# Ten feed-forward input blocks with a fifth seven-product pair, and four weight sums by adding transfers

## The chip, the cores and the metric

The kernel runs on one core of a Trainium2 chip. A core has a matrix engine (TensorE, PE in the profile, with PEld for its weight loads), a vector engine (VectorE, DVE), a scalar engine (ScalarE, ACT), a general engine (GpSimd, POOL) and an engine for synchronisation (SyncE, SP), which here issues the plain transfers. Sixteen DMA engines move the data. SBUF and PSUM are the core's on-chip memories; matmuls write to PSUM, in banks of 128 x 512 float32. The metric is device time in microseconds for one call, smaller is better; the time of a kernel is the median of its runs.

## The reference, cut to what matters

An encoder block on 256 tokens of width 2048, all in float32: three token mixers side by side (one of them attends to 256 memory tokens), an output projection, and a SwiGLU feed-forward part.

```python
h = rms_norm(x, g_mix)
proj = h @ w_in                       # q, k, v of three mixers, and gates
mkv = rms_norm(mem, g_mem) @ w_mem_kv # keys and values of the memory
...
merged = gates[0] * (oa @ w_br_a) + gates[1] * (ob @ w_br_b) + gates[2] * (oc @ w_br_c)
x = x + merged @ w_o
hf = rms_norm(x, g_ffn) @ w_ffn_in                              # 2048 -> 2 * 5632
x = x + (silu(hf[..., :D_FF]) * hf[..., D_FF:]) @ w_ffn_out     # 5632 -> 2048
```

## The kernel before

**Number format.** A float32 product is done as three matmuls of a faster format: each operand is split into a high part (a rounded copy, made by ACT) and a low part (the rest, made by a DVE subtraction), and the kernel sums high x high, high x low and low x high. In `mul` (line 476) these are the three matmuls of one 128-row k-tile, one 128-token tile and 512 columns. Weights are split on the chip, as they arrive: `halves` (line 425) makes the high part of a 512 KB tile (ACT, line 438), and `low` (line 445) issues the subtraction (DVE, line 448) one step later.

**Weights.** They come in tiles of 512 KB: two k-tiles of 128 rows by 512 columns, u = 0 to 7 for a width of 2048. `load` (line 218) takes the first of a list of free places (eleven once `more` and `both` are there) and issues the transfer on SP's queue, in program order; `release` appends the place to the list once the tile's last split has been issued, and a transfer into it waits for that split. Split tiles have five buffers. A weight tile that needs adding to another gets that by an accumulating transfer, which GpSimd's queue issues (line 535): the second matrix is read from memory and added to what lies in the tile.

**Pairs of column blocks.** From the gates on, `pair` (line 450) computes two neighbouring column blocks at once, c = 0 and 1, for both token tiles: a 2 x 2 arrangement of outputs. `whole` (line 499) is the ordinary product of one weight tile with both token tiles: four k-tile products, 12 matmuls. A "double" takes two weight tiles u and their k-tiles in a 2 x 2 form and does, for two pairs of k-tiles at once, seven products in place of eight (Strassen's method in Winograd's form). The seven are called X, W, P, Y, Q, Z, H; each is 6 matmuls for the double. Their weight operands are b11, a sum t = b11 + b12 (the accumulating transfer), then P: t + b22 (DVE, line 581), Y: b21, Q: t - b11 (line 583), Z: b22, H: t + b21 (line 585). In an FFN input block two doubles (u = 0 to 3) are done so, u = 4 to 7 as wholes; it has 28 + 32 = 60 k-tile products of three matmuls. Sums of the banks between the phases are lines 558 to 567.

**Order.** A string lists the steps of a pair, such as

```python
STEPS_FFN = ("l0 l1 X0 X1 . r0 W0 r1 W1 P0 P1 . Y0 Y1 . Q0 Q1 .", "Z0 Z1 D4 H0 D5 H1 D6 D7", "d4 d5 d6 d7")
```

l0 and l1 load b11 and t and issue t's accumulating transfer; r0 and r1 load b22 and b21; D and d are wholes of column blocks 1 and 0. The third string is the tail: its steps take the dots of the next pair's first string, so that the end of a block lies among the beginning of the next. `run` (line 616) takes the steps in this order: a step's weights are made ready (sums, ACT's high part, the deferred low part), and its matmuls are issued four steps later. ACT, DVE and PE run these instructions in the order written.

**FFN.** `feeding` runs input blocks 0 to 3, two output pairs, blocks 4 to 7, two output pairs, blocks 8 to 10, two output pairs. An input block computes 512 columns of both halves of the SwiGLU, then silu (line 983), the product with the other half (line 986), transposes and a split into `hT`. The seven products also need sums of the activations; `transposed` and `token_sums` make them into `room` for the doubles.

**The beginning.** The first products are the memory's keys and values, then the queries, keys and values of x (`whole_k`, all wholes). The two column blocks of these use banks of tags "at" and "tp". `take_slots` (line 656) takes them out of PSUM: keys at once, values (`V`, lines 135 and 136, split straight out of PSUM) only once the row scale r is known, which needs rows that are loaded later. `load_T` (line 261) fetches the transposed inputs, 256 KB for two k-tiles, the first one in two halves of 128 KB between the halves of the first weight tile. Eight matmuls of an identity matrix run on PE ahead of the first product.

**Slots.** Small things (rows, one-hot tables, copies of banks, av) take one of five slots of 4 KB per partition, the s4 pool.

Of the kernel before, what the change touches and what calls it, by code (L numbers as in the profile page):

```python
# [18 lines left out]
P = 128  # L19
# [41 lines left out]
STEPS_FFN = ("l0 l1 X0 X1 . r0 W0 r1 W1 P0 P1 . Y0 Y1 . Q0 Q1 .", "Z0 Z1 D4 H0 D5 H1 D6 D7", "d4 d5 d6 d7")  # L61
STEPS_LAST = ("l0 l1 X0 X1 . r0 W0 . r1 W1 . P0 P1 . Y0 Q0 Q1 Y1", "Z0 Z1 H0 H1 D4 D5", "d4 d5")
# [41 lines left out]
def encoder_block(ctx: ExitStack, tc: tile.TileContext, a: dict, out: bass.AP):  # L104
# [111 lines left out]
    def load(src, k0, nk, parts=1, between=None):  # L216
# [5 lines left out]
        for k in range(0, nk, nk // parts):  # L222
            n = nk // parts
            if k and between:
                between(k0 + k)
            nc.sync.dma_start(out=raw[:, k:k + n].rearrange("p k n -> p (k n)"),
                              in_=src[k0 // PK][:, c + k * NC:c + (k + n) * NC])
# [33 lines left out]
    def load_T(src, g, tag):  # L261
# [3 lines left out]
        raws, fetched, have = {}, set(), set()  # L265

        def get(k, fetch=False, n=2):
# [5 lines left out]
            if not fetched.intersection(ks):  # L273
                nc.sync.dma_start(out=raws[k0][:, ks[0] - k0:ks[0] - k0 + n],
                                  in_=src[k0 // 2].rearrange("p (k s) -> p k s", s=S)[:, ks[0] - k0:ks[0] - k0 + n])
            fetched.update(ks)
# [26 lines left out]
    def transposed(src, dst, g=None, lag=1, also=None):  # L303
# [3 lines left out]
        for h in range(2):  # L307
# [14 lines left out]
            if also is not None:  # L322
# [5 lines left out]
                else:  # L328
                    for k in range(2):
                        nc.scalar.activation(to[:, k], of[:, k], AF.Copy, scale=g(2 * h + k))  # L330
        if also is not None:
            token_sums(full, also)

    def token_sums(full, to):


        raw = s4([P, 2, 4, P], "fraw")
# [12 lines left out]
    for _ in range(8):  # L350
# [74 lines left out]
    def halves(*srcs, each=None):  # L425
# [5 lines left out]
        n = 0  # L431
        for v in srcs:
            v = v.unsqueeze(1) if len(v.shape) == 2 else v
            o = slice(n, n + v.shape[1])
            if each:
                low(0)
                each(n)
            nc.follow(nc.scalar.activation(hi[:, o], v, AF.Copy))  # L438
            due.append((lo[:, o], v, hi[:, o].bitcast(F32)))
# [5 lines left out]
    def low(n):  # L445

        while len(due) > n:
            nc.follow(nc.vector.tensor_sub(*due.pop(0)))  # L448

    def pair(src, lhs, lists, done, doubles=(), forms=None, operand=None, fresh="", early=False, by_halves=False):  # L450
# [12 lines left out]
        left = {"Y": 2 * nd + 2 * wholes["d"], "X": 6 * nd, "V": 2 * nd + 2 * wholes["d"],  # L463
                "W": 4 * nd + 2 * wholes["D"], "Q": 2 * wholes["D"]}
# [3 lines left out]
        stops = {"X": [left["X"] - n * nd for n in (2, 4, 6)], "W": [left["W"] - 2 * nd]}  # L468
# [30 lines left out]
        def whole(u, c):  # L499
            def ready():  # L500
                last_kind[0] = ""
                parts = 2 if operand and u + c == 0 else 1
                if operand and c == 0:
                    operand(2 * u, True, 3 - parts)
                raw = load((src(u, c),), 0, PK, parts, lambda k: operand(k, True, 1))
# [31 lines left out]
        def begin2(m):  # L537
            j = doubles[m][1]
            raws[m].update({"b22": load((src(j, 1),), 0, PK), "b21": load((src(j, 0),), 0, PK)})
# [6 lines left out]
        def phase_end(kind, hi):  # L546
            seen[kind] = seen.get(kind, 0) + 1
            if seen[kind] < nd:
# [19 lines left out]

        def seventh(kind, m):
            of = {"X": "b11", "W": "t", "Y": "b21", "P": "t", "Z": "b22", "Q": "b11", "H": "b21"}[kind]  # L570
            bk = {"P": "X", "Q": "X", "H": ends[0][1], "Z": "W"}.get(kind, kind)
            needs = {"Y": "X", "P": "X", "Z": "P", "Q": "P", "H": "Q"}

            def ready():
                r = raws[m]
                raw = r[of]
# [7 lines left out]
                elif kind == "H":  # L584
                    nc.follow(nc.vector.tensor_add(raw, r["t"], raw))
                hi, lo = halves(raw)
                for n in {"Q": ["b11"], "Z": ["b22"], "H": ["t", "b21"]}.get(kind, ()):
                    release(r.pop(n))

                def products():  # L590
                    assert kind not in needs or seen.get(needs[kind], 0) == nd, (kind, seen)
                    assert kind != "Z" or seen["W"] == nd
                    for i in range(2):
# [4 lines left out]
                        mul(bk, st, hi[:, i], lo[:, i])  # L598
# [5 lines left out]
        def step(o):  # L604
# [5 lines left out]
            if kind in "lr":  # L610
                return lambda: (begin if kind == "l" else begin2)(n)
# [492 lines left out]
```

## Time and profile before

| | |
|---|---|
| Time, median of 3 runs | 1365.81 us (1365.35 to 1368.44) |
| Profiled execution | 1366.78 us, of which the span is 1365.0 us |
| PE busy | 1354.4 us (99%) |
| DVE busy | 1157.6 us (85%) |
| ACT busy | 855.6 us (63%) |
| Transfers | 301.18 MB, 221 GB/s on the mean |
| of them accumulating (queue q0) | 24.12 MB, 9.4% of the DMA engines' span |
| One FFN input block (735.44 to 777.21) | 41.77 us, PE busy throughout |

The span runs from the first to the last instruction of the core; the profiled execution's time has 1.78 us around it. Busy shares are averages over stages that differ. A row of a window lists its bounds and length, then for PE, PEld, DVE, ACT and POOL the busy time with the number of instructions, then PE's granted clock, the busy share of the DMA engines and GB/s. A row of a timeline is start, duration, engine, line, operation, what it writes and reads, and in brackets how long the engine sat idle before it and what it waited for. Matmuls overlap, so that their durations (0.39 us for one of 512 columns) are longer than their distance.

### The profile page before, as it was taken

Reading aid. Unit: us, or ns where it says so; the run is one execution under the profiler, and the core shown is the slowest. Engines: PE = TensorE matmul, PEld = TensorE weight load, DVE = VectorE, ACT = ScalarE, POOL = GpSimd, SP = SyncE. Lnnn points to the kernel's source line nnn. Section 1 sums busy time; section 2 is a strip of 40 time slices with the busy share of each in tenths; the row PEclk is TensorE's granted clock in tenths of the full one; section 3 lists DMA queues with packets and bytes.
Section 4 is the critical chain, followed back from the end, with each engine's and each line's share of the span. In section 5 each row is a group of like instructions: output and inputs, shape, how many; then the busy total and the mean of one; then the engine's idle time right before and its main releaser. Section 6 shows DMA issues by size and latency. Waiting matters only on the chain.

```text
span 1365.0 us, 17319 instructions
## 1 busy us (share of the span) xinstructions
PE 1354.4 (99%) x6170; PEld 1122.6 (82%) x6170; DVE 1157.6 (85%) x1412; ACT 855.6 (63%) x1110; POOL 53.1 (4%) x60
## 2 busy tenths in 40 slices
PE   9989999999999999999999999999999999999998
PEld 7878888888888888888888888888888888888887
DVE  6768876778879779878899998888999889989997
ACT  7766656556656565656776666555666655566664
POOL 0010001000000000000000000000000000000000
PEclk9989999999999999999999999999999999999999
DMA  9967555546785594785578666787666786666873
GB/s 358 351 186 220 155 153 171 171 132 212 256 289 190 183 312 141 264 286 148 191 232 270 187 213 212 244 262 234 202 227 203 249 272 191 227 219 213 278 220 103
DMA packets 86486, 301.18 MB, mean 221 GB/s; under 512 B 9792, under 2 KB 12608, under 8 KB 86144
## 3 DMA queue, kind: packets, MB, share of 16 engines
q1 hardware_dynamic: 79632, 275.94, 58.2%
q0 software_dynamic: 6624, 24.12, 9.4%
q8 instruction: 48, 0.79, 0.2%
q14 instruction: 38, 0.31, 0.1%
q10 hardware_dynamic: 144, 0.02, 0.0%
HBM read 297.17 MB, written 2.88 MB: 220 GB/s over the span
## 4 chain that ended last, share of the span: by engine, by line
PE 94%; DVE 3%; DMA 1%; ACT 1%; issue 1%; SPq 0%; DVEq 0%; ACTq 0%
PE mmX L79 28%; PE mmW L79 19%; PE mm L79 16%; PE mmY L79 15%; PE mmQ L79 11%; DVE wlo L448 2%; PE tp L79 1%; PE sc L79 1%; PE o L79 1%; DMA raw<-in_w_br 1%; ACT whi L438 1%; PE pT L79 1%; PE hT L79 0%; DMA raw<-in_w_mem 0%; DVE raw L583 0%
## 5 line engine op out<-in xcount | busy, mean ns | idle before, releaser
L438 ACT ACTIVATE whi<-raw 128x1024 fp32r<-128x1024 f32 (+1 forms) x363 | 376.9, 1055 | 231.3 <-PE mmQ L79 52.3
L448 DVE TENSOR_TENSOR wlo<-raw,whi 128x1024 fp32r<-128x1024 f32 (+1 forms) x363 | 437.9, 1220 | 84.6 <-ACT whi L438 81.0
L79 PE MATMUL mm<-whi,xT 128*128 128x512 f32 x640 | 205.3, 396 | 3.9 <-DVE V L136 3.9
L79 PEld LDWEIGHTS mm<-whi,xT 128*128 128x128 f32 x640 | 120.6, 190 | 29.3 <-DVE V L136 4.4
L438 ACT ACTIVATE whi<-both 128x1024 fp32r<-128x1024 f32 x101 | 106.5, 1055 | 58.6 <-DVE both L583 18.1
L133 DVE TENSOR_TENSOR wlo<-raw,whi 128x1024 fp32r<-128x1024 f32 x82 | 103.1, 1261 | 42.1 <-ACT whi L132 41.7
L448 DVE TENSOR_TENSOR wlo<-both,whi 128x1024 fp32r<-128x1024 f32 x101 | 123.1, 1222 | 11.6 <-ACT whi L438 10.8
L448 DVE TENSOR_TENSOR wlo<-more,whi 128x1024 fp32r<-128x1024 f32 x89 | 108.7, 1223 | 24.0 <-ACT whi L438 23.0
L438 ACT ACTIVATE whi<-more 128x1024 fp32r<-128x1024 f32 x89 | 93.9, 1058 | 54.2 <-PE mmQ L79 15.4
L79 PE MATMUL mm<-wlo,xT 128*128 128x512 f32 x320 | 126.5, 395 | 0.0
L132 ACT ACTIVATE whi<-raw 128x1024 fp32r<-128x1024 f32 x82 | 86.6, 1061 | 60.4 <-PE mm L79 43.5
L79 PE MATMUL mmW<-whi,forms 128*128 128x512 f32 x368 | 122.1, 391 | 0.0
L79 PE MATMUL mmX<-whi,forms 128*128 128x512 f32 x368 | 122.1, 391 | 0.0
L79 PE MATMUL mmX<-whi,x1T 128*128 128x512 f32 x352 | 120.9, 389 | 0.0
L79 PE MATMUL mmY<-whi,x1T 128*128 128x512 f32 x264 | 89.1, 389 | 0.0
L79 PEld LDWEIGHTS mmW<-whi,forms 128*128 128x128 f32 x368 | 69.1, 188 | 14.2
L79 PEld LDWEIGHTS mmX<-whi,forms 128*128 128x128 f32 x368 | 69.1, 188 | 14.2
L79 PEld LDWEIGHTS mmX<-whi,x1T 128*128 128x128 f32 x352 | 66.1, 188 | 13.7
L79 PE MATMUL mmX<-wlo,forms 128*128 128x512 f32 x184 | 71.7, 389 | 0.0
L79 PE MATMUL mmW<-wlo,forms 128*128 128x512 f32 x184 | 71.7, 389 | 0.0
L79 PEld LDWEIGHTS mm<-wlo,xT 128*128 128x128 f32 x320 | 60.8, 190 | 11.7
L79 PE MATMUL mmX<-wlo,x1T 128*128 128x512 f32 x176 | 68.5, 389 | 0.0
(277 smaller groups left out, 2592.9 us busy)
## 6 DMA issues: line engine op xcount, KB each, us to landing
raw<-in_w_ffn SPq DMA_DIRECT2D x116, 512.0 KB, 5.9
raw<-in_w_gate SPq DMA_DIRECT2D x66, 512.0 KB, 5.0
raw<-in_w_qkv SPq DMA_DIRECT2D x64, 512.0 KB, 4.2
raw<-in_w_ffn_out SPq DMA_DIRECT2D x54, 512.0 KB, 7.1
both<-in_w_ffn SPq DMA_DIRECT2D x33, 512.0 KB, 8.1
more<-in_w_ffn SPq DMA_DIRECT2D x27, 512.0 KB, 6.5
raw<-in_w_o SPq DMA_DIRECT2D x22, 512.0 KB, 4.9
both<-in_w_ffn_out SPq DMA_DIRECT2D x20, 512.0 KB, 5.3
```

Of the source, the lines that this page charges most:

```text
L79: ins = op(*args, **kw)
L132: nc.scalar.activation(hi, src, AF.Copy)
L133: nc.vector.tensor_sub(lo, src, hi.bitcast(F32))
L438: nc.follow(nc.scalar.activation(hi[:, o], v, AF.Copy))
L448: nc.follow(nc.vector.tensor_sub(*due.pop(0)))
```

## The change

Five things change.

1. Ten of the eleven FFN input blocks (n = 1 to 10) get a new step list, `STEPS_FFN5`. In it weight tile u = 6, until now the wholes d6 and D6, becomes a "single": its two k-tiles are one more 2 x 2 form and get seven products in place of eight. They come in four parts, each with its own ready step: S1 (X and W), S2 (P and Y), S3 (Q and Z), S4 (H). Its operands are halves of the two tiles t and b1, and so are its sums (DVE, half tiles) and splits; the sum t is again made by an accumulating transfer, of one half, which step `s0` issues behind its loads. A block then has 59 k-tile products.
2. In these blocks the sum of H of the two doubles is no longer a DVE addition: after Q's subtraction, steps `a0` and `a1` add b21 to t by an accumulating transfer. The tile b21 is loaded at Y instead of at r0 and r1, and given back at once.
3. The activation sums of the single lie in a tile `lone`, which holds one of the s4 slots from the projection to the end. It is filled once, at the last transpose of the projection, by two ACT copies, three small DVE operations and one split.
4. `take_slots` copies the value part of the banks to a tile `vraw` (an s4 slot) at once with two ACT instructions, where the scale is not known yet (the memory's); V is then split from there.
5. `load_T` fetches all pieces as 256 KB; the first weight tile still comes in halves. Eleven identity matmuls run ahead, not eight.

The low parts of a step that has two halves are kept together in a list; their order does not change.

```diff
@@ -59,6 +59,8 @@
 STEPS_FFN = ("l0 l1 X0 X1 . r0 W0 r1 W1 P0 P1 . Y0 Y1 . Q0 Q1 .", "Z0 Z1 D4 H0 D5 H1 D6 D7", "d4 d5 d6 d7")
+STEPS_FFN5 = ("l0 l1 X0 s0 X1 S1 . W0 W1 r0 P0 . r1 P1 S2 Y0 Y1 . Q0 a0 Q1 a1 S3",
+              "Z0 Z1 D4 H0 D5 H1 D7 S4", "d4 d5 d7")
 STEPS_LAST = ("l0 l1 X0 X1 . r0 W0 . r1 W1 . P0 P1 . Y0 Q0 Q1 Y1", "Z0 Z1 H0 H1 D4 D5", "d4 d5")
@@ -213,7 +215,7 @@

-    def load(src, k0, nk, parts=1, between=None):
+    def load(src, k0, nk, parts=1):

@@ -221,8 +223,6 @@
             n = nk // parts
-            if k and between:
-                between(k0 + k)
             nc.sync.dma_start(out=raw[:, k:k + n].rearrange("p k n -> p (k n)"),
@@ -262,7 +262,7 @@
         tiles = [s8([P, 4, 2, S], tag) for _ in range(KT // 4)]
-        raws, fetched, have = {}, set(), set()
+        raws, have = {}, set()

@@ -270,10 +270,7 @@
                 raws[k0] = early.tile([P, 2, S], F32, name="rawT", bufs=4)
-            if not fetched.intersection(ks):
-                nc.sync.dma_start(out=raws[k0][:, ks[0] - k0:ks[0] - k0 + n],
-                                  in_=src[k0 // 2].rearrange("p (k s) -> p k s", s=S)[:, ks[0] - k0:ks[0] - k0 + n])
-            fetched.update(ks)
+                nc.sync.dma_start(out=raws[k0], in_=src[k0 // 2].rearrange("p (k s) -> p k s", s=S))
             if not fetch:
@@ -300,7 +297,7 @@

-    def transposed(src, dst, g=None, lag=1, also=None):
+    def transposed(src, dst, g=None, lag=1, also=None, single=None):

@@ -328,13 +325,20 @@
                         nc.scalar.activation(to[:, k], of[:, k], AF.Copy, scale=g(2 * h + k))
+            if single is not None and h == 0:
+                one, of = s4([P, 1, 4, P], "ffull"), tp.rearrange("p (k s) -> p k s", s=S)
+                for k in range(2):
+                    nc.scalar.activation(one[:, 0, 2 * k:2 * k + 2].rearrange("p t s -> p (t s)"), of[:, k], AF.Copy,
+                                         scale=g(k) if g else 1.0)
+                token_sums(one, single)
         if also is not None:
...

-        raw = s4([P, 2, 4, P], "fraw")
+        n = full.shape[1]
+        raw = s4([P, n, 4, P], "fraw")
         nc.vector.tensor_sub(raw[:, :, :2], full[:, :, :2], full[:, :, 1::2])
@@ -347,7 +351,7 @@
     idle = bank("idle", "tp")
-    for _ in range(8):
+    for _ in range(11):
         nc.tensor.matmul(idle[:, :P], lhsT=ident, rhs=ident, start=True, stop=True)
@@ -429,14 +433,16 @@
         n = 0
+        due.append([])
         for v in srcs:
...
                 low(0)
+                due.append([])
                 each(n)
             nc.follow(nc.scalar.activation(hi[:, o], v, AF.Copy))
-            due.append((lo[:, o], v, hi[:, o].bitcast(F32)))
+            due[-1].append((lo[:, o], v, hi[:, o].bitcast(F32)))
             n += v.shape[1]
@@ -445,9 +451,10 @@
         while len(due) > n:
-            nc.follow(nc.vector.tensor_sub(*due.pop(0)))
-
-    def pair(src, lhs, lists, done, doubles=(), forms=None, operand=None, fresh="", early=False, by_halves=False):
+            for part in due.pop(0):
+                nc.follow(nc.vector.tensor_sub(*part))
+
+    def pair(src, lhs, lists, done, doubles=(), forms=None, operand=None, fresh="", early=False, by_halves=False, single=None):

@@ -460,12 +467,15 @@
         nd, wholes = len(doubles), {c: sum(o[0] == c for o in order) for c in "dD"}
-        left = {"Y": 2 * nd + 2 * wholes["d"], "X": 6 * nd, "V": 2 * nd + 2 * wholes["d"],
-                "W": 4 * nd + 2 * wholes["D"], "Q": 2 * wholes["D"]}
+        ns = "S1" in order
+        units, phases = 2 * nd + ns, nd + ns
+        added = {int(o[1:]) for o in order if o[0] == "a"}
+        left = {"Y": units + 2 * wholes["d"], "X": 3 * units, "V": units + 2 * wholes["d"],
+                "W": 2 * units + 2 * wholes["D"], "Q": 2 * wholes["D"]}
         if not early:
...
         ends = "YV" if early else "YX", "WQ"
-        stops = {"X": [left["X"] - n * nd for n in (2, 4, 6)], "W": [left["W"] - 2 * nd]}
+        stops = {"X": [left["X"] - n * units for n in (1, 2, 3)], "W": [left["W"] - units]}
         ps, raws, seen, ended = {}, {}, {}, set()
@@ -501,8 +511,8 @@
                 if operand and c == 0:
-                    operand(2 * u, True, 3 - parts)
-                raw = load((src(u, c),), 0, PK, parts, lambda k: operand(k, True, 1))
+                    operand(2 * u, True)
+                raw = load((src(u, c),), 0, PK, parts)
                 if parts == 2:
@@ -536,7 +546,52 @@
             j = doubles[m][1]
-            raws[m].update({"b22": load((src(j, 1),), 0, PK), "b21": load((src(j, 0),), 0, PK)})
+            raws[m]["b22"] = load((src(j, 1),), 0, PK)
+            if m not in added:
+                raws[m]["b21"] = load((src(j, 0),), 0, PK)
+
+        def fourth(m):
+            nc.gpsimd.dma_start(out=raws[m]["t"].rearrange("p k n -> p (k n)"), in_=src(doubles[m][1], 0),
+                                accum_op=ALU.add)
+
+        def begin_single(_):
+            t = load((src(single[0], 1),), 0, PK)
+            raws["s"] = {"t": t, "b1": load((src(single[0], 0),), 0, PK)}
+            nc.gpsimd.dma_start(out=t[:, 0], in_=src(single[0], 0)[:, :NC], accum_op=ALU.add)
+
+        def at_single(kind):
+            k = 2 * single[0]
+            return {"X": lambda: at(k, 0), "Y": lambda: at(k + 1, 0), "H": lambda: at(k + 1, 1),
+                    "W": lambda: single[1](0), "P": lambda: single[1](1), "Z": lambda: single[1](2),
+                    "Q": lambda: single[1](3)}[kind]()
+
+        def part(n):
+            kinds = ("XW", "PY", "QZ", "H")[n - 1]
+
+            def ready():
+                t, b1 = raws["s"]["t"], raws["s"]["b1"]
+                if last_kind[0] == "S" + str(n - 1):
+                    low(0)
+                last_kind[0] = "S" + str(n)
+                if n == 2:
+                    nc.follow(nc.vector.tensor_add(t[:, 0], t[:, 0], t[:, 1]))
+                elif n == 3:
+                    nc.follow(nc.vector.tensor_sub(b1[:, 0], t[:, 0], b1[:, 0]))
+                elif n == 4:
+                    nc.follow(nc.vector.tensor_add(b1[:, 1], t[:, 0], b1[:, 1]))
+                hi, lo = halves(*((b1[:, 0], t[:, 0]), (t[:, 0], b1[:, 1]), (b1[:, 0], t[:, 1]), (b1[:, 1],))[n - 1])
+                if n == 4:
+                    release(t)
+                    release(b1)
+
+                def products():
+                    for i, kind in enumerate(kinds):
+                        ordered(kind)
+                        mul(bank_of(kind), at_single(kind), hi[:, i], lo[:, i])
+                        phase_end(kind, hi)
+                    ending()
+                return products
+            return ready

@@ -545,7 +600,7 @@
             seen[kind] = seen.get(kind, 0) + 1
-            if seen[kind] < nd:
+            if seen[kind] < phases:
                 return
@@ -566,13 +621,21 @@

+        def bank_of(kind):
+            return {"P": "X", "Q": "X", "H": ends[0][1], "Z": "W"}.get(kind, kind)
+
+        def ordered(kind):
+            needs = {"Y": "X", "P": "X", "Z": "WP", "Q": "P", "H": "Q"}.get(kind, "")
+            assert all(seen.get(k, 0) == phases for k in needs), (kind, seen)
+
         def seventh(kind, m):
-            of = {"X": "b11", "W": "t", "Y": "b21", "P": "t", "Z": "b22", "Q": "b11", "H": "b21"}[kind]
-            bk = {"P": "X", "Q": "X", "H": ends[0][1], "Z": "W"}.get(kind, kind)
-            needs = {"Y": "X", "P": "X", "Z": "P", "Q": "P", "H": "Q"}
+            of = {"X": "b11", "W": "t", "Y": "b21", "P": "t", "Z": "b22", "Q": "b11",
+                  "H": "t" if m in added else "b21"}[kind]

...
                 r = raws[m]
+                if kind == "Y" and m in added:
+                    r["b21"] = load((src(doubles[m][1], 0),), 0, PK)
                 raw = r[of]
@@ -581,21 +644,21 @@
                     nc.follow(nc.vector.tensor_sub(raw, r["t"], raw))
-                elif kind == "H":
+                elif kind == "H" and m not in added:
                     nc.follow(nc.vector.tensor_add(raw, r["t"], raw))
                 hi, lo = halves(raw)
-                for n in {"Q": ["b11"], "Z": ["b22"], "H": ["t", "b21"]}.get(kind, ()):
+                for n in {"Y": ["b21"] * (m in added), "Q": ["b11"], "Z": ["b22"],
+                          "H": ["t"] + ["b21"] * (m not in added)}.get(kind, ()):
                     release(r.pop(n))
...
                 def products():
-                    assert kind not in needs or seen.get(needs[kind], 0) == nd, (kind, seen)
-                    assert kind != "Z" or seen["W"] == nd
+                    ordered(kind)
                     for i in range(2):
...
                               "Z": lambda: forms(m, i, 2), "Q": lambda: forms(m, i, 3)}[kind]()
-                        mul(bk, st, hi[:, i], lo[:, i])
+                        mul(bank_of(kind), st, hi[:, i], lo[:, i])
                     phase_end(kind, hi)
@@ -607,8 +670,10 @@
                 return whole(n, "dD".index(kind))
-            if kind in "lr":
-                return lambda: (begin if kind == "l" else begin2)(n)
+            if kind in "lras":
+                return lambda: {"l": begin, "r": begin2, "a": fourth, "s": begin_single}[kind](n)
+            if kind == "S":
+                return part(n)
             return seventh(kind, n)
@@ -667,6 +732,13 @@
                 nc.vector.tensor_reduce(ss[:, :, :n], sq[:, :, :n], axis=AX.X, op=ALU.add)
+        held = [ps[t][:, n * HD:].rearrange("p (n d) -> p n d", d=HD) for t in range(T)]
+        if n < len(slots) and name not in known:
+            raw = s4([P, T, 4, HD], "vraw")
+            with tc.high_priority():
+                for t in range(T):
+                    nc.scalar.activation(raw[:, t, n:], held[t], AF.Copy)
+            held = [raw[:, t, n:] for t in range(T)]
         if name not in known:
@@ -676,7 +748,7 @@
                 for t in range(T):
-                    split(v[:, 0, t], v[:, 1, t], ps[t][:, i * HD:(i + 1) * HD], r[:, 0, t:t + 1])
+                    split(v[:, 0, t], v[:, 1, t], held[t][:, i - n], r[:, 0, t:t + 1])
         if n:
@@ -957,9 +1029,11 @@
                         room.extend(form_room(3))
+                        lone.append(s4([P, 1, 2, 4, P], "lone", F32R))
                     yield from transposed(xc, lambda k, m: (x1T[n + c][:, 0, k], x1T[n + c][:, 1, k]),
                                           lambda k: gT[:, 2, 4 * (n + c) + k:4 * (n + c) + k + 1], 2,
-                                          also=room[2 + n + c] if n == 0 else None)
+                                          also=room[2 + n + c] if n == 0 else None,
+                                          single=lone[0] if n + c == 3 else None)
                 start(urgent(later()))
@@ -992,8 +1066,8 @@
                     start(urgent(later()))
-                yield pair(lambda u, c, n=n: a["w_ffn"][n][2 * u + 1 - c], x1l, STEPS_FFN if n else STEPS_FFN0, hidden,
-                           TWO, by_room(lambda: room[2:]))
+                yield pair(lambda u, c, n=n: a["w_ffn"][n][2 * u + 1 - c], x1l, STEPS_FFN5 if n else STEPS_FFN0, hidden,
+                           TWO, by_room(lambda: room[2:4]), single=(6, lambda f: [lone[0][:, 0, i, (f + 1) % 4] for i in range(2)]))
             pairs = (STEPS_LAST, STEPS_LAST2) if last else (STEPS_FFN, STEPS_FFN)
```

More of the change, by code (lines that the diff above doesn't have):

```diff
@@ L866, in encoder_block @@
     home = lambda n: big if n == 3 else tail
-    mT, x1T, x, room = {}, [], [], []
+    mT, x1T, x, room, lone = {}, [], [], [], []
     ss1 = const.tile([P, T, 4], F32, name="ss1")
```

## The prediction

> **What bounds the kernel now.** I read the page's head, slices and chain first, then windows around the places where PE is not full, then one FFN input block instruction by instruction.
>
> ```profile
> span 1365.0 us, 17319 instructions
> PE 1354.4 (99%) x6170; PEld 1122.6 (82%) x6170; DVE 1157.6 (85%) x1412; ACT 855.6 (63%) x1110; POOL 53.1 (4%) x60
> PEclk9989999999999999999999999999999999999999
> PE 94%; DVE 3%; DMA 1%; ACT 1%; issue 1%; SPq 0%; DVEq 0%; ACTq 0%
> ```
>
> PE is busy for 99% of the span and is 94% of the chain. So a change pays if it takes matmuls away without starving PE, or closes one of the few gaps. The only slice in mid-kernel with a lower granted clock is the third (68 to 102 us). The profiled execution took 1366.78 us, 1.78 more than its span; the median of the runs is 1365.81, 0.97 less. I sum against 1366.78 and subtract 0.97 at the end.
>
> The windows give PE busy, PEld, DVE, ACT, POOL, then granted clock and DMA share:
>
> ```profile
> 4.00:12.00 8.00, 6.92 (x24) 4.89 (x23) 4.63 (x8) 4.90 (x8) 0.00 (x0) 1.00 0.97 354
> 73.00:77.40 4.40, 0.47 (x3) 0.04 (x2) 3.92 (x11) 4.40 (x12) 0.00 (x0) 0.81 1.01 340
> 77.40:83.00 5.60, 5.60 (x14) 4.45 (x15) 1.41 (x9) 4.03 (x10) 2.38 (x1) 0.54 0.55 163
> 83.00:100.00 17.00, 17.00 (x78) 13.63 (x78) 10.62 (x34) 9.57 (x19) 0.00 (x0) 1.00 0.46 151
> 735.44:777.21 41.77, 41.77 (x192) 34.58 (x190) 38.71 (x39) 27.70 (x31) 1.15 (x2) 1.00 0.70 231
> 1183.00:1207.00 24.00, 24.00 (x107) 19.90 (x106) 19.73 (x19) 13.57 (x15) 1.72 (x2) 1.00 1.00 332
> 1207.00:1220.00 13.00, 13.00 (x59) 10.76 (x58) 12.12 (x11) 8.32 (x10) 0.00 (x0) 1.00 0.18 59
> ```
>
> See three things. Around 73 us PE stands still, then runs at a clock of 0.54. An FFN input block (row 735.44 to 777.21) is PE from end to end, with DVE busy 38.71 of 41.77 us. Inside such a block the DMA engines are full for 24 us around the block's border and nearly idle (0.18) for 13 us behind it.
>
> **The change, part by part.**
>
> *Fewer matmuls.* 78 matmuls in the 17.00 us of row 83 to 100 are 0.22 us each; the rows below (1244.26 to 1246.97, twelve matmuls) give 0.226. Ten blocks issue 59 x 3 matmuls in place of 60 x 3: 30 fewer, **-6.8 us**.
>
> *The wait at 73 us.* V's rows on line 136:
>
> ```profile
> L136 DVE SCALAR_TENSOR_TENSOR V<-mmW,scales,V x4: 344/345/347, 67.6 to 77.0; 128x128 fp32r<-128x128 f32 x4
>   PE mm L79: 3.9, 1
> 73.04 0.39 PE L79 MATMUL mm<-whi,xT 128*128 128x512 f32 x1
> 77.36 0.79 PE L79 MATMUL mm<-whi,xT 128*128 128x512 f32 x1 [3.93 <-DVE V L136]
> 78.38 1.05 PE L79 MATMUL mm<-whi,xT 128*128 128x512 f32 x2
> 79.66 1.05 PE L79 MATMUL mm<-whi,xT 128*128 128x512 f32 x2
> 83.04 0.61 PE L79 MATMUL mm<-whi,xT 128*128 128x512 f32 x2
> ```
>
> V of mem is split out of its two banks piece by piece until 77.2; the next column block needs those banks from 73.27 (73.04 and a pitch of 0.226). It starts at 77.36: 4.1 us lost. Then three matmuls take 1.28 us (78.38 to 79.66), 0.427 each against 0.226; over the 14 matmuls and 5.60 us of the row 77.40 to 83, 5.60 - 14 x 0.226 = 2.4 us. After the change two ACT copies of 128x512 empty the banks at once, at about 66 us, seven us before PE asks. With no standstill there is no slow stretch: **-6.6 us**. What could be late next is the weights: ACT is full from 73.00 to 77.40 (4.40 of 4.40), but in the 5.60 us after it is busy 4.03 while PE crawls, so it keeps up with what PE takes (one split of 1.06 us for twelve matmuls, 2.7 us). I cost the rest at nothing, at most +3.3, half of the gain.
>
> *The start.* DMA share is 0.97 from 4 to 12 us and PE idle 1.08 us: landings set the pace. The same bytes in another order, and three more idle matmuls, move the first real matmul but not the last landing. I take **-0.3 us**, between -0.8 and +0.8 (most of the 1.08, and the same the other way).
>
> *The `lone` sums* are two copies on ACT, three small DVE operations and a split, once, beside a full PE: nothing, at most 1 us.
>
> *DVE per FFN block.* Rows of one block:
>
> ```profile
> 1227.77 1.22 DVE L585 TENSOR_TENSOR raw<-more,raw 128x1024 f32<-128x1024 f32 x1
> 1228.91 1.22 DVE L448 TENSOR_TENSOR wlo<-raw,whi 128x1024 fp32r<-128x1024 f32 x1
> 1230.05 0.68 DVE L986 TENSOR_TENSOR av<-av,mmY 128x512 f32<-128x512 f32 x1
> 1230.64 0.68 DVE L986 TENSOR_TENSOR av<-av,mmX 128x512 f32<-128x512 f32 x1
> 1231.24 1.22 DVE L448 TENSOR_TENSOR wlo<-raw,whi 128x1024 fp32r<-128x1024 f32 x1
> ```
>
> From start to start a full tile takes 1.14 us and a half tile 0.60. A block loses two sums of line 585 and two splits (d6, D6), 4 x 1.14, and gains seven half splits and three half sums, 10 x 0.60: +1.4 us on 38.71, and the period falls to 41.1. DVE still fits, but has nearly nothing left to catch up with. From S1 to Q1, DVE has 15 full operations, 3 halves and about 4 halves of other work: 17.1 + 4.2 = 21.3 us; PE has 96 matmuls, 21.8 us. A delay that reaches DVE at S1 stays until Q1.
>
> *Transfers.* Accumulating transfers go from two to five a block.
>
> ```profile
> q1 hardware_dynamic: 79632, 275.94, 58.2%
> q0 software_dynamic: 6624, 24.12, 9.4%
> both<-in_w_ffn SPq DMA_DIRECT2D x33, 512.0 KB, 8.1
> raw<-in_w_ffn SPq DMA_DIRECT2D x116, 512.0 KB, 5.9
> raw<-in_w_ffn POOLq DMA_DIRECT2D x12, 512.0 KB, 8.9
> DMA to landing us min/median/max: 5.8/8.9/11.0
> 1226.85 3.64 SPq L79 DMA_DIRECT2D raw<-in_w_ffn  x2
> 1230.53 0.43 SPq L79 DMA_DIRECT2D more<-in_w_ffn  x1
> 1232.49 0.33 SPq L79 DMA_DIRECT2D raw<-in_w_ffn  x1
> 1244.26 0.39 PE L79 MATMUL mmW<-whi,x1T 128*128 128x512 f32 x1
> 1246.97 0.39 PE L79 MATMUL mmX<-whi,x1T 128*128 128x512 f32 x1
> ```
>
> Queue q0 moved 46 tiles of 0.524 MB in 9.4% of the span, 2.79 us each of all engines; q1 526 tiles in 58.2%, 1.51 each. A block needed 16 x 1.51 + 2 x 2.79 = 29.7 us of the engines; afterwards 24.2 + 4 x 2.79 + 1.4 = 36.7 of 41.1. It fits on the mean, and part of it falls well: the two new full sums start at Q0 and Q1, in the end of the 13 us with a share of 0.18, and b21 moves out of the full stretch into that gap.
>
> The Trainium skill ("DMA: Bandwidth & Descriptors", Issuing engines are not separate DMA queues) says that transfers started by different engines run on the same 16 engines and interleave; so the sums that leave DVE are paid in loads that come later, and the full stretch of 24 us bears that out.
>
> What falls badly is `s0`, whose half sum is the last of five in POOL's queue and the last thing that S1 needs. Its t tile is the fifth load behind the block's border. In the trace H0 gives back two places when its split (1228.91) ends, at about 1230.1, and loads go out at 1230.16 (the second of the row at 1226.85, which ends at 1230.49) and at 1230.53. Afterwards H0 gives back only t, so s0's t waits for the split of D5 (1231.24 + 1.22) and goes out as the load at 1232.49 does. The block's X0 began at 1246.97; with S4 (3 matmuls) in place of D6 (12) it comes 2.04 earlier, 1244.93. So t is issued at -12.4 us against X0; landing 8.1 later (the slower group, since the engines are full) at -4.3; the accumulate, 8.9 less 1.4 for half the bytes, lands at +3.2. Then ACT's half (0.60, as DVE's) and DVE's half (0.68) end at +4.5, and d4's split behind it, 1.14, at +5.6. PE wants d4's low part at +4.3 (X0, X1, S1: 18 matmuls, and one more). **Late by 1.3 us**, and DVE has no room to make it up. Bounds: with t landing in 5.9 and the accumulate at its fastest (5.8 - 1.4), nothing is late; with the accumulate at its slowest (11.0 - 1.4), 3.4 us. I take the 1.3 of the medians. It holds where the block ahead is of the new kind too: n = 2, 3, 5, 6, 7, 9, 10, seven blocks: **+9.1 us** (0 to 24). The blocks behind an output block or FFN0 have two accumulates fewer in front of s0, and their place at 1230.5.
>
> Sum: -6.8 - 6.6 - 0.3 + 9.1 = -4.6: 1362.2 in the profiled execution, **1361.2 us** as the median.
>
> **The rivals.**
>
> *Nothing is late* (s0 lands by +1.9): -13.7, **1352.1**. For it: the engines have 4 us a block to spare, and b21 leaves the full stretch. Against it: the median of 8.9 was taken with two sums in the queue, not five.
> The same page of the Trainium skill (Anatomy of one DMA, SWDGE path) fits 2.0 us plus bytes over 436 GB/s for a transfer from this queue, an estimate of 2.6 us for 256 KB, by which s0 would land at -1.7 and this rival would be the result. The trace speaks against it, with 5.8 us at the least for 512 KB.
>
> *The accumulates queue up* and the stall outgrows the saving: slower than before. Its place is S1 (and Q1, behind a0) in the seven blocks; it costs the lateness of s0 times seven, and decides from 13.7 / 7 = 1.96 us a block on. With 2.7 us, between my 1.3 and the bound of 3.4, that is 18.9 - 13.7 = +5.2, **1371**. For it: q0 tiles cost the engines 1.85 times a plain one, and five in 25 us are 12.6 us of them; against it: they begin in the idle stretch.
>
> *Another wait takes the place of V's*: `vraw` holds one of the five slots of the s4 pool over the time when rows and one-hot tables are loaded through the same queue as the weights; half of the 6.6 comes back: **1364.5**. For it: ACT full from 73 to 77; against it: split weights stand ready when PE stops, since PE resumes without a load wait.
>
> *DVE becomes the bound* through its own work: 38.71 + 1.4 = 40.1 of 41.1. Not by itself; it is what keeps the lateness alive.
>
> **How the numbers follow.** Forecast (0.6 to 1.6 us late a block) 0.42; nothing late 0.20; queueing beyond 2.35 a block 0.20; V's gain half lost 0.10; lateness between 1.6 and 2.35 0.08. A measurement of this kernel can tell about 0.2% (2.7 us) from no change. Faster: 0.42 + 0.20 = 0.62; the same 0.10 + 0.08 = 0.18; slower 0.20. The range runs from the case without stalls (1352) to a little beyond the queueing case (1372).
>
> **What would show it.** Right: no PE gap between 60 and 100 us and a clock of 9 in the third slice; PE gaps of about 1 us ahead of S1's second half or d4's low part, once a block, in blocks 2, 3, 5 to 7, 9, 10 and not in 1, 4, 8; idle ACT ahead of S1's half split, ended by the accumulate. Wrong: block periods of 41.1 throughout (first rival), gaps at W, Q or H as well (the engines short of bandwidth, not one late tile), or a new gap near 75 to 100 us.

## The result, and the profile after

The changed kernel takes 1412.95 us (median of 4 runs, 1410.34 to 1413.55) against 1365.89 us before: a ratio of 1.0337, with a 95% interval of 1.0321 to 1.0352. It is 47 us slower, outside the forecast range. The page of the changed kernel, the same lines as before (span, busy times, granted clock, chain, the queue of the accumulating transfers):

```profile
span 1411.8 us, 17489 instructions
PE 1370.3 (97%) x6146; PEld 1121.7 (79%) x6146; DVE 1168.3 (83%) x1476; ACT 869.9 (62%) x1165; POOL 79.1 (6%) x90
PEclk9999999999999999999999999999999999999999
DVE 12%; PE 11%; DMA 6%; issue 3%; ACT 2%; SPq 0%; ACTq 0%; DVEq 0%
q0 software_dynamic: 10944, 37.23, 14.2%
```

PE has 24 fewer records, yet is busy 16 us longer, and it idles 41.5 us of the span where it idled 10.6 (1411.8 - 1370.3 and 1365.0 - 1354.4). The chain, which could be followed back over a third of the span only, no longer runs through PE alone: DVE has as much of it, and DMA and ACT come into it.

**Where the time went.** The start of each block's first X matmul, found by counting matmuls in PE's timeline, gives the stages. "Without a wait" is the period before the change, less or plus the matmuls that left or joined the block (0.2266 us each). Blocks 1, 4 and 8 gain nine matmuls each, since the tail of the pair ahead, which lies among their beginning, still has its old length; an output pair behind a new block has twelve fewer.

| Stage | Before | After | Without a wait |
|---|---|---|---|
| start of the first gate block | 321.11 | 313.34 | |
| second gate block | 49.43 | 50.97 | 49.43 |
| FFN block 0 | 42.76 | 45.07 | 42.76 |
| FFN block 1 | 41.77 | 48.40 | 43.81 |
| FFN blocks 2, 3 | 41.77 | 47.32, 45.59 | 41.09 |
| FFN block 4 | 40.80 | 48.47 | 42.84 |
| FFN blocks 5, 6, 7 | 41.77 | 48.44, 48.20, 46.73 | 41.09 |
| FFN block 8 | 40.80 | 44.29 | 42.84 |
| FFN blocks 9, 10 | 41.77 | 47.29, 46.87 | 41.09 |
| last output pair but one, last with the end | 36.33, 39.93 | 36.03, 40.51 | 33.61, 39.93 |

The beginning gave 7.8 us and the matmuls 6.8. The ten blocks lost 54.5 us (the sum of "after" less "without a wait"), 30.2 of them with PE idle; FFN block 0 lost 2.3, the second gate block 1.5, the last two output pairs 3.0: together 46.7, and the spans differ by 46.8.

**The beginning** went as forecast. Windows of the changed kernel (bounds, length, busy time by engine, granted clock, DMA share):

```profile
73.00:77.40 4.40, 4.40 (x22) 3.62 (x21) 2.55 (x3) 4.40 (x12) 0.30 (x1) 1.00 1.06 345
77.40:83.00 5.60, 5.60 (x26) 4.67 (x25) 4.86 (x8) 5.07 (x8) 2.12 (x1) 1.00 0.60 203
1022.03:1070.23 48.20, 44.82 (x186) 35.59 (x185) 39.91 (x44) 29.15 (x36) 4.33 (x5) 0.93 0.74 221
...
1025.12:1028.53 3.41, 1.39 (x6) 0.57 (x4) 1.03 (x2) 2.17 (x4) 0.00 (x0) 1.00 0.61 244
...
1028.53:1035.36 6.83, 5.80 (x14) 4.18 (x14) 6.17 (x6) 4.88 (x7) 0.00 (x0) 0.50 0.24 79
```

PE is full from 73 to 83 us at a clock of 1.00. The third row is FFN block 6: 3.4 us of its loss of 7.1 are idle PE (48.20 - 44.82). The other 3.7 (44.82 - 41.09) are mostly matmuls at a lower clock: the fourteen in the last row, where the granted clock is 0.50, take 0.43 us each (1.28 us for three) in place of 0.2266, which is 2.8 us. Not every block loses clock. Six of the ten (1, 2, 4, 5, 6 and 9) have a stretch at 0.50, with 74 matmuls in all, about 15 us; blocks 3, 7 and 10 stay at 1.00 and still lose 4.5 to 5.8 us each.

**The loss of one block**, in ACT's timeline around the border to block 6 (X0 at 1022.03; line 444 makes high parts, line 1057 is silu):

```profile
1019.18 0.63 ACT L444 ACTIVATE whi<-raw 128x512 fp32r<-128x512 f32 x1 [0.60 <-DMA raw<-in_w_ffn]
1026.36 0.63 ACT L444 ACTIVATE whi<-both 128x512 fp32r<-128x512 f32 x1 [6.54 <-DMA both<-in_w_ffn]
1026.89 0.67 ACT L1057 ACTIVATE av<-mmW,scales 128x512 f32<-128x512 f32 x1
1027.46 0.68 ACT L1057 ACTIVATE av<-mmQ,scales 128x512 f32<-128x512 f32 x1
1028.03 1.05 ACT L444 ACTIVATE whi<-raw 128x1024 fp32r<-128x1024 f32 x1
```

ACT stands still for 6.54 us until s0's sum lands, at +4.3 us against X0. PE wanted the high part made from it at +3.4. What the wait costs stands behind it: silu of the block before, which empties the banks W and Q, and the split of d4, whose tile had lain there since 1022.9. PE, same kernel:

```profile
1027.62 0.50 PE L81 MATMUL mmW<-whi,lone 128*128 128x512 f32 x1 [2.02 <-ACT av L1057]
1029.14 0.79 PE L81 MATMUL mmY<-whi,x1T 128*128 128x512 f32 x1 [0.56 <-ACT whi L444]
1030.40 0.79 PE L81 MATMUL mmY<-wlo,x1T 128*128 128x512 f32 x1 [0.47 <-DVE wlo L455]
1030.99 1.05 PE L81 MATMUL mmY<-whi,x1T 128*128 128x512 f32 x2
1033.55 1.05 PE L81 MATMUL mmX<-whi,x1T 128*128 128x512 f32 x2
```

What S1's second half waits for last is not its own weights (ready at 1026.99) but silu (until 1027.56), because it starts in the bank W; then d4 waits for its high part, and for its low part. In blocks 4 and 8, behind an output block, it is a DVE addition to x that stands behind the wait in place of silu. The matmul at 1029.14 already takes 0.79 us where one takes 0.39: the clock halved at 1028.53, and until 1035.3 three matmuls take 1.28 us. The Trainium skill ("TensorE: Matmul & The Clock Gate", The HAM clock gate) puts the halving down to an idle window of about 3.4 us; the trace differs, since PE had been idle for only 2.02 of the 3.41 us ahead (the row from 1025.12), and for 2.0 to 2.9 of them in the six blocks.

The waits for this one tile over the whole kernel (the line of s0's accumulating transfer, who waited for it, and issue to landing; then the same of the full sums of l0 and l1):

```profile
  ACT whi L444: 53.4, 10
DMA to landing us min/median/max: 7.2/9.4/11.0
...
DMA to landing us min/median/max: 5.6/9.1/10.9
```

Ten waits, one a block, 53.4 us in all. And half the bytes land no sooner here: 9.4 us against 9.1. Against its block's X0 the sum landed between +0.7 (block 8) and +5.3 us (block 5), at +2.9 on the median, so that block 6 is one of the later ones.

### The profile page after: what moved, and what is told of

It reads as the page before. It is cut to its first block, busy times and chain, and to the rows that moved or that the text cites. A ratio compares the mean times of both kernels' runs of the same rounds, so it can differ in the third digit from the quotient of the medians.

```text
span 1411.8 us, 17489 instructions
## 1 busy us (share of the span) xinstructions
PE 1370.3 (97%) x6146; PEld 1121.7 (79%) x6146; DVE 1168.3 (83%) x1476; ACT 869.9 (62%) x1165; POOL 79.1 (6%) x90
## 5 line engine op out<-in xcount | busy, mean ns | idle before, releaser
L444 ACT ACTIVATE whi<-raw 128x1024 fp32r<-128x1024 f32 (+1 forms) x396 | 391.5, 1008 | 270.3 <-DMA raw<-in_w_ffn 48.2
L455 DVE TENSOR_TENSOR wlo<-raw,whi 128x1024 fp32r<-128x1024 f32 (+1 forms) x396 | 454.7, 1164 | 116.7 <-ACT whi L444 112.7
L81 PE MATMUL mm<-whi,xT 128*128 128x512 f32 x640 | 202.4, 393 | 0.0
L444 ACT ACTIVATE whi<-both 128x1024 fp32r<-128x1024 f32 (+1 forms) x103 | 101.2, 984 | 76.7 <-DMA both<-in_w_ffn 19.2
L455 DVE TENSOR_TENSOR wlo<-both,whi 128x1024 fp32r<-128x1024 f32 (+1 forms) x103 | 116.7, 1134 | 31.7 <-ACT whi L444 31.3
L444 ACT ACTIVATE whi<-more 128x1024 fp32r<-128x1024 f32 (+1 forms) x104 | 104.2, 1006 | 57.1 <-DVE more L644 16.8
L455 DVE TENSOR_TENSOR wlo<-more,whi 128x1024 fp32r<-128x1024 f32 (+1 forms) x104 | 120.5, 1161 | 15.3 <-ACT whi L444 14.3
```

The costliest lines, as they stand in the source:

```text
L81: ins = op(*args, **kw)
L455: nc.follow(nc.vector.tensor_sub(*part))
```

## The experiments

The two theories at the start: **(A)** one late tile, s0's sum, holds up ACT and what stands behind it; **(B)** the DMA engines are short of bandwidth through the new sums of H. **(C)**, later: DVE has no room from d4 to Q1. Each run had the kernel before beside it on the same chip.

| Kernel | us, median | Ratio to before, 95% interval |
|---|---|---|
| e1 beginning only | 1359.63 | 0.9936 to 0.9969 |
| e2 S1 behind W1 | 1388.99 | 1.0147 to 1.0191 |
| e3 t of the single by DVE | 1366.66 | 0.9996 to 1.0014 |
| e4 sums of H by DVE | 1427.56 | 1.0431 to 1.0481 |
| e5 sums of H by transfer, no single | 1360.14 | 0.9940 to 0.9970 |
| e7 W of the single apart | 1374.70 | 1.0037 to 1.0070 |
| e8 S1 behind W1, d5 ahead of P0 | 1380.49 | 1.0089 to 1.0120 |
| e9 lone made, not used | 1362.76 | 0.9966 to 0.9986 |
| e10 as e7, d4 first | 1375.04 | 1.0050 to 1.0084 |
| e11 s0 ahead of l1 | 1372.16 | 1.0027 to 1.0061 |
| e12 as e11, half sums left out | 1362.81 | 0.9952 to 0.9978 |
| e13 high part by DVE | 1398.49 | 1.0213 to 1.0254 |

### e1: the beginning alone

The changed kernel with `STEPS_FFN` in the ten blocks and no `lone`.

> Only the parts at the beginning (value copies, whole first pieces, eleven idle matmuls); all feed-forward blocks as before. The two theories: (A) the loss of the changed kernel is one late tile, the half sum of s0, for which ACT waits in order at S1 with silu and the split of d4 queued behind it; (B) the loss is the DMA engines' bandwidth, used up by the two new sums of H. Both expect the same here: the first gate block began 7.8 us earlier in the changed kernel than before (313.79 against 321.56), so 1357 to 1359 us. If it is over 1362, the beginning's gain depends on the rest or is given back in the gates (one wait of 0.9 us was new there).

1359.63 us, 0.6 above the range, and every FFN period is that of before. The beginning is worth 6.7 us by itself, and the feed-forward part gives nothing back.

### e3 and e4: one of the two kinds of sums undone

```diff
 e3, begin_single:
-            nc.gpsimd.dma_start(out=t[:, 0], in_=src(single[0], 0)[:, :NC], accum_op=ALU.add)
 e3, part:
-                if n == 2:
+                if n == 1:
+                    nc.follow(nc.vector.tensor_add(t[:, 0], t[:, 0], b1[:, 0]))
+                elif n == 2:
 ...
 e4:
-"... Y0 Y1 . Q0 a0 Q1 a1 S3"
+"... Y0 Y1 . Q0 Q1 S3"
```

> The changed kernel with the single's sum t made by a DVE half addition (0.69 us) at S1 in place of s0's accumulating transfer; the two sums of H stay transfers. (A) expects S1 to wait for a plain load only (s0's tiles landed at -6.3 and -3.0 us against X0), no standstill, 1354 to 1368 us. (B) expects four of the five sums to keep the engines full, d4's and later tiles late, 1385 us or more.

> The changed kernel with the sums of H of the two doubles by DVE again (b21 loaded at r0 and r1), the single's t still by an accumulating transfer. (A) expects the loss to stay, since blocks 1 and 4, which had no sum of H ahead of them, lost 7 us each: 1390 to 1415 us. (B) expects it to go: 1352 to 1362 us.

They speak for (A). Without s0's accumulate 46 of the 47 us are gone, though four full sums a block are still transfers; the ten blocks lose 9.2 us in place of 54.5. With fewer transfers, but s0's kept, it gets worse: 1427.6, above the range that (A) gave (the 7 us in its text are against the periods of before; without a wait blocks 1 and 4 lose 4.6 and 5.6). ACT and POOL of e4 around a border (X0 at 1023.76):

```profile
1024.32 0.86 POOL L560 DMA_DIRECT2D both<-in_w_ffn  x1 [7.10 <-DMA both<-in_w_ffn]
1031.85 0.63 ACT L444 ACTIVATE whi<-both 128x512 fp32r<-128x512 f32 x1 [2.02 <-DMA both<-in_w_ffn]
```

The accumulate starts at +0.6 us, in the changed kernel at -5.8, and over the ten blocks s0's sum lands at +6.1 on the median, not at +2.9. In e4 b21 sits in its place from r0 until H, so s0's load gets a place later: -9.8 in place of -13.4. The changed kernel gives b21's place back at once, so the sums by transfer helped here. How much of e4's loss comes from DVE's two sums was not tried.

### e5: the sums of H by transfer, without the single

```diff
+STEPS_FFNA = ("l0 l1 X0 X1 . r0 W0 r1 W1 P0 P1 . Y0 Y1 . Q0 a0 Q1 a1 .", "Z0 Z1 D4 H0 D5 H1 D6 D7", "d4 d5 d6 d7")
```

> The kernel of e1 (beginning only, 1359.6 us) with the sums of H of the ten blocks by adding transfers and no single: four accumulates a block, b21 loaded at r0 and r1 as before. (A) one late tile at S1 is the cause, so with no S1 nothing waits: 1358 to 1361 us. (B) bandwidth: waits at d4 or W, over 1370 us.

1360.14, as e1, with 34.6 MB through the accumulating queue. Block 6 of e5:

```profile
991.85:1033.62 41.77, 41.77 (x190) 34.57 (x188) 36.71 (x37) 27.83 (x32) 3.46 (x4) 1.00 0.81 253
```

DMA share up from 0.70 to 0.81, PE full, DVE two sums lighter: the second part of the change costs nothing, and (B) is refuted for it. That the fifth sum's bytes are not the cause either is shown by e11 below, which has all five.

### e2, e7, e8: S1 later

```diff
-"l0 l1 X0 s0 X1 S1 . W0 W1 r0 P0 . r1 P1 S2 Y0 Y1 . Q0 a0 Q1 a1 S3"
+"l0 l1 X0 s0 X1 W0 . W1 S1 r0 P0 . r1 P1 S2 Y0 Y1 . Q0 a0 Q1 a1 S3"       (e2)
+"l0 l1 X0 s0 X1 S1 . W0 W1 S5 r0 P0 . r1 P1 S2 Y0 Y1 . Q0 a0 Q1 a1 S3"    (e7: S1 only X, S5 is W)
+"l0 l1 X0 X1 . s0 W0 W1 r0 S1 . P0 r1 P1 S2 Y0 Y1 . Q0 a0 Q1 a1 S3"       (e8)
```

> The changed kernel with step S1 moved behind W1 (5.4 us of matmuls later), same transfers. (A) expects the waits at S1 and d4 to go, FFN block periods of 41.1 to 42.5 us and 1352 to 1366 us. (B) expects the wait to move to other steps, the periods to stay above 45 and 1390 us or more.

> The changed kernel with S1 taken apart: X of the single (which needs only a plain load) stays at its place, W (which needs s0's sum) comes behind W1, 5.4 us later, as a step of its own. In e2 S1 as a whole was moved and PE waited for the copy of X's bank ahead of P0, which here keeps its cover. (A) expects ACT not to wait any more and silu and d4 not to queue: periods of 41.1 to 42.5 us, 1353 to 1364 us, with 2 us lost in the first block as in e3. (B) expects 1385 us or more.

> The changed kernel with s0 issued behind d4's load and S1 as a whole moved behind W1, but with the whole d5 between S1 and P0, which covers the copy of X's bank by 2.7 us. (A) expects the wait ahead of P0 of e2 to go and d4 to be on time: 1353 to 1364 us. If the copy of the bank was not what e2 waited for, it stays near 1385 us.

All three missed their ranges, on the high side. e2 comes close to the 1390 us that (B) named, but what its PE waits for is no transfer. The wait at S1 goes in each; in e2 and e8 a new one comes. In e2 PE waits ahead of P0 in all ten blocks for the copy of X's bank:

```profile
PE mmX L81 <- ACT mmY L613: 22.6, 10, 3.0
```

I took that for missing cover and put the 2.7 us of d5 between (e8). The wait stayed, in eight blocks and up to 1.8 us, and its rows say why (ACT, then PE):

```profile
1015.60 0.61 ACT L444 ACTIVATE whi<-more 128x512 fp32r<-128x512 f32 x1
1016.12 0.58 ACT L613 ACTIVATE mmY<-mmX 128x512 f32<-128x512 f32 x1
...
1016.75 0.50 PE L81 MATMUL mmX<-whi,forms 128*128 128x512 f32 x1 [1.73 <-ACT mmY L613]
```

A step's matmuls are issued four steps after its weights are made ready, so the copy that follows S1 stands in ACT's order behind the splits of the next four steps; in e8 (d5, P0, P1, S2) the last of them is two steps behind P0, and S2's split waits for a buffer that PE is to free. So here X must end four steps ahead of P0; matmul time between them is no help. e7 does that: no bank waits, no wait at S1, and still 1374.7.

### e11: the same transfers in another order

```diff
-"l0 l1 X0 s0 X1 S1 . W0 W1 ..."
+"l0 s0 l1 X0 X1 S1 . W0 W1 ..."
```

> The changed kernel with s0 moved ahead of l1 in the order of steps: the same transfers, the single's sum second of the three in the queue and its loads two places earlier; S1 stays at its place. (A) expects the accumulate to land at about +1 us in place of +4.3, in time for S1's second half at +3.4: the wait of ACT goes, with what queues behind it, and the time falls to 1358 to 1370 us with e3's DVE waits left. If transfers beside each other all come later whatever their order, S1 still waits: over 1390 us.

1372.16: moving one step two places forward takes 41 us off. s0's sum lands at -0.8 us in block 6, and the line of its transfer now reads:

```profile
  ACT whi L444: 8.8, 7
```

53.4 us of ACT's waiting have become 8.8, and the ten blocks lose 13.3 us in place of 54.5. So 41 us of the loss were the place of one transfer in POOL's queue and its loads' place in SP's. The time is 2 us above the range given.

### e13: who stands behind the wait

```diff
+            if second and n:
+                low(0)
+                due.append([])
+                nc.follow(nc.vector.tensor_copy(hi[:, o], v))
+            else:
...
```

> The changed kernel with the high part of the half that waits for s0's sum (S1's second half) made by DVE in place of ACT; order and transfers as they are. Now DVE waits for the transfer, and ACT goes on to silu and d4. If what made a tile 1 us late cost 7 us a block is that silu and d4's split stand behind the wait in ACT's order, a good part goes: 1380 to 1398 us (the transfer is as late as before, and DVE's own queue still waits). If the late tile alone is the cost, it stays at 1408 to 1418 us.

1398.49: a tile as late (over the ten blocks +3.4 on the median against +2.9), waited for by DVE, costs 14.5 us less. Silu now runs 1.8 us before X0 to 0.2 after it (X0 at 1007.36), and d4's high part follows as its tile lands:

```profile
1005.52 0.69 ACT L1062 ACTIVATE av<-mmW,scales 128x512 f32<-128x512 f32 x1 [0.60 <-PE mmW L81]
1006.88 0.69 ACT L1062 ACTIVATE av<-mmQ,scales 128x512 f32<-128x512 f32 x1 [0.67 <-PE mmQ L81]
1008.82 1.06 ACT L449 ACTIVATE whi<-raw 128x1024 fp32r<-128x1024 f32 x1 [1.25 <-DMA raw<-in_w_ffn]
...
1010.74 0.43 DVE L447 CAST whi<-both 128x512 fp32r<-128x512 f32 x1 [4.64 <-PE mmX L81]
```

The row of DVE names PE as what ended the wait, but s0's sum landed at 1010.7. The time is 0.5 us above the range given. At least a quarter of the 54.5 us was ACT's queue behind the wait, since 14.5 us go when ACT no longer waits. DVE now has its own queue behind the same tile; how the rest divides was not tried.

### e10 and e12: what is left

```diff
+"l0 l1 X0 X1 . s0 S1 W0 W1 S5 r0 . P0 r1 P1 S2 Y0 Y1 . Q0 a0 Q1 a1 S3"      (e10, S5 as in e7)
 e12, part of e11:
-                if n == 2:
-                    nc.follow(nc.vector.tensor_add(t[:, 0], t[:, 0], t[:, 1]))
...
```

> e7 lost about 1.4 us a block at Q1 and up to 1.1 at d4, where DVE ran without a pause from d4's late load (landing at +0.2 us) to Q1. Here s0's loads come behind d4's, the X part of the single behind d4, its W part behind W1, and d5 stands ahead of P0, so that the copy of X's bank keeps four steps. If DVE's missing lead is what is left (C: it starts late because d4 is late, and then has no room), d4 lands 3 to 6 us earlier and the block periods fall to 41.1 to 42: 1355 to 1364 us. If DVE's work itself is too much in this stretch wherever it starts, it stays at 1368 to 1376 us.

> The kernel of e11 (1372.2 us) without the three half sums of the single in S2, S3 and S4 (left out: the single's products are then of unsummed operands): 1.8 us of DVE work a block less, 1.2 of it in the stretch from d4 to Q1. If DVE's own work in this stretch is what is left in e7, e10 and e11 (C), the waits at Q1 (1.4 us) and d5 shrink or go: 1361 to 1367 us. If it is order or landing, 1370 to 1374 us.

e10 stayed at 1375.0 although d4's tile landed at -7.4 us: it is not a late start. e12, with 1.8 us of DVE work a block less, came to 1362.8, and its ten blocks lose 4.5 us where those of e11 lose 13.3. DVE's own work is most of what is left. Of the last 4.5 us the record shows only where they lie: in blocks 3, 6, 7 and 10 (0.9 to 1.4 us each), where PE waits for a low part of DVE near the start of the block. In e7 from d4's split to Z1's (25.76 us), then in e12 over block 6 (third busy time is DVE):

```profile
1002.24:1028.00 25.76, 24.55 (x110) 19.80 (x109) 24.78 (x27) 17.44 (x22) 1.73 (x2) 1.00 0.67 206
...
993.90:1035.86 41.96, 41.71 (x186) 33.86 (x185) 36.51 (x40) 28.25 (x36) 4.33 (x5) 1.00 0.84 257
```

DVE is busy 24.78 of 25.76 us there, and PE waits at Q1, for 1.2 us (25.76 - 24.55). In e12 the waits at Q1 are gone and the period of block 6 is 41.96; that of block 2 is 41.09.

### e9: the tile lone

> The kernel of e1 with the sums of the single made and held in the tile lone but not used: its computation and its slot alone. In all kernels with the single the first block takes 45.1 us in place of 42.8. If lone does that, 1361 to 1363 us and a first block of 45 us; if the step list behind it does, 1359.6 us.

1362.76, and FFN block 0 takes 45.06 us with lone (first row) and 42.76 without (e1, second row):

```profile
659.13:704.19 45.06, 43.33 (x197) 35.20 (x196) 42.00 (x61) 31.34 (x45) 1.73 (x2) 1.00 0.59 182
...
657.71:700.47 42.76, 42.76 (x198) 35.33 (x197) 40.53 (x57) 30.31 (x42) 1.74 (x2) 1.00 0.64 197
```

Making it costs 2.3 us once, in a block whose DVE is full as well (42.00 of 45.06). Whether its work or its slot does it was not tried. The second gate block also took 50.7 in e9; it varies between 49.4 and 51.0 over these kernels, with a wait at D4, and why stays open.

## Why the prediction was wrong

- **The wait at 73 us and the start**: right. Forecast 6.9 us (the two parts of the wait, 4.1 and 2.4, add up to 6.5, not 6.6); 7.8 in the trace of the changed kernel, 6.7 by the medians of e1.
- **Fewer matmuls**: right, 6.8 us; in e12 undisturbed blocks of the new kind come to 41.09 us.
- **The sums of H and bandwidth**: right that they fit (e5). That they are paid in later loads was not: e5 takes as long as e1. The third rival's slot of `vraw` did nothing.
- **s0's sum at S1**: the place was right, the term was mis-sized. Seven blocks were charged with the lateness alone, 1.3 us each, +9.1 in all, with a bound of 24. These seven lost 42.8 us, 4.5 to 7.35 each, and all ten 54.5; 41 us of that go when the sum comes earlier (e11), and 45 when there is no such transfer (e3).
  - *The landing* did not fail, but by luck. Forecast at +3.2; in the seven blocks +1.8 to +5.3, median 3.1. The accumulate began earlier than forecast (median -6.2, not -4.3) and took longer (9.8 us, not 7.5: the discount of 1.4 us for half the bytes did not show). The two errors cancel.
  - *What stands behind the wait* is the step that failed. The sum let only the tile's own split and d4's follow, and put d4's low part at +5.6. In the trace of block 6 it ends at +8.3, of which 1.1 us is that block's later landing: two silu instructions stand between in ACT's order, and PE waits for them too. The prediction named no instruction queued behind the waiting one but d4's. It did not price the clock either: about 2.8 of the 7.1 us in block 6, about 15 of the 54.5.
  - *Which blocks* failed too. It excepted 1, 4 and 8, since fewer sums stood ahead. They lost 4.6, 5.6 and 1.4: three accumulates (l0, l1, s0) are enough.
- **DVE has no room**: right as a mechanism, and taken as cover for a lateness only. In e10, where d4 and s0 were in time, the blocks still lost 1.4 us on the mean (0 to 4.5). So the rival "DVE becomes the bound", to which the text gave no chance, is most of what stops this change once s0 is in time (e12).
- **lone** was costed at nothing to 1 us; it took 2.3 in FFN block 0 (e9).

The rival on the slower side (accumulates queue up, 1371 us) was nearest, but with the wrong price: not the lateness of s0 times seven, but that lateness plus what stands in two engines' orders behind it, plus the clock.

The best version measured is e1: 1359.63 us, ahead of both kernels. With 6.8 us to win, the single costs more than that in every order tried; even without its half sums (e12) it gains nothing on e1.

## What to carry to other kernels

Price a wait by the queue behind it: list what the waiting engine does next, and who waits for that; in block 6 a sum that landed 0.9 us after PE wanted its high part cost 7.1 us. Before moving work from a busy engine to a transfer, find the transfer's place in its queue and let the most urgent one go first: one step in another order was worth 41 us. Count the clock as well: in this kernel, 2 us of idle PE within 3.4 us were followed by 3.4 to 6.8 us at half speed.

## What had not been expected of the hardware

- In the changed kernel an accumulating transfer of 256 KB took as long as one of 512 KB from issue to landing: 7.2 to 11.0 us (median 9.4) against 5.6 to 10.9 (9.1). It is no rule: in e11 the medians are 8.5 and 9.2, in e4 7.5 and 9.2.
- One pause of 2.02 us (1025.60 to 1027.62) was enough to bring PE's granted clock from 1.00 to 0.50, for 6.83 us (1028.53 to 1035.36).
- 10.5 MB more through the accumulating queue (24.1 to 34.6 MB) cost no time at all where no instruction waited in order for one of them.
